# A planned attention schedule: the third branch's first pair goes by halves of the queries, and one gate projection moves to the end of the dense work

## The chip, the cores and the metric

One kernel runs on one core of a Trainium2 chip. The metric is the device time of one execution in microseconds (us); the median of three executions stands for a kernel. TensorE (PE) does the matmuls, VectorE (DVE), ScalarE (ACT) and GpSimd (POOL) the elementwise work, and SyncE's queue (SP) starts most transfers.

## The reference, cut to what matters

One decoder layer over 1024 tokens of width 1024. A projection of `x` feeds three attention branches of 8 heads of width 64, and three gates of width 1024.

```python
proj = einsum('bsd,dc->bsc', x, w_in)
o_a = dsa_attention(...)            # top 256 keys of each query by an indexer's score, then softmax
o_b = forgetting_attention(...)     # softmax with a cumulative forget bias
o_c = stick_breaking_attention(...)
up = einsum('ibsw,iwd->bsid', stack([o_a, o_b, o_c]), w_branch)
merged = sum(up * sigmoid(gates), axis=2)
y = einsum('bsd,de->bse', merged, w_out)
x = layer_norm(alpha * x + y);  x = layer_norm(alpha * x + squared_relu_mlp(x))
```

## The kernel before, in words

**Attention.** The kernel runs the branches in the order Fox (forgetting), Stick, Dsa (top-k); the third one here is Dsa. A branch has four pairs of heads, so the pairs are numbered 0 to 11 and the third branch's first pair is pair 8. The queries come in 8 row blocks of 128. A `Unit` is one head and two neighbouring row blocks: `u` from 0 to 3 has the blocks 2u and 2u+1. For each block, `qk` makes a row of scores in PSUM (tag "l", two banks; a row longer than 512 takes both), and `rows` turns it into weights `p`: a DVE operation adds the bias `bt`, reads the scores and gives the row's minimum `nm`; ACT takes the exponential with its sum `sm`; DVE inverts `sm`; POOL multiplies. Then `tr` transposes `p` (tag "t", two banks), ACT and DVE split it into `ph` and `pl`, and `pv` multiplies with `v` into tag "o".

**Selection.** `select` finds for every query its 256th largest indexer score by a bitwise search, in the background of the first two branches. At the end it handles the row blocks 2 to 7 one after the other: five DVE operations (`eq`, the scan `rk`, `eq`, `eq`, and the one that rewrites `score[i]`), and an `iota` on POOL. From `score[i]` POOL makes the bias `bt` of block i. Before a Dsa unit's scores are emitted, the loop `while selected[0] <= 2 * un.u + n` emits whatever is missing of the selection up to that block; `fill_gap` may emit more of it into a gap that the planner sees on DVE.

**Dense work.** A queue of projection tasks (`dq`) fills PE between attention steps: the q, k and v projections of the pairs (`st` is the split copy of a q or k block, which SP's queue then lays out as `qa`, `qb`, `ka`, `kb`) and the 24 gate blocks. One `gate` is a `proj_T`: 8 x 2 x 3 = 48 matmuls of 128x512 into two of the three "d" banks, then two ACT copies `g_` and two stores to `g_scratch` from ACT's queue. `GATES[4 * n + p - 1]` says how many gates follow the projections of pair 4n+p; those left over follow at the end. `dense_upto` lets the queue run ahead to the projections of the next pair. All weights of dense tasks arrive as `wraw` through SP's queue.

**Order.** `Plan` keeps an estimated clock for each engine. `drive` emits the attention step whose inputs and buffers are due, and a piece of dense work where none is due in time. The engines then run their own instructions strictly in the resulting order.

**After attention.** `load_wb` and `load_o` fetch the first branch's output (`oraw`, two halves that DVE adds, then `oh` and `ol` by ACT and DVE) into space that attention has given back. `dq.finish(len(dq.tasks))` runs what is left of the dense queue. Then the up-projections begin: for each of 8 blocks 24 matmuls with `oh`, `ol` and the weights `wbhi`, `wblo`.

In the trace almost everything has the line 138, in which the planner's helper issues an instruction; instructions are therefore told by their tiles.

Of the kernel before, what the change touches and what calls it, by code (L numbers as in the profile page):

```python
# [30 lines left out]
NPAIR = NH // 2  # L31
# [9 lines left out]

GATES = (3, 1, 3, 0, 2, 0, 2, 3, 2, 1, 2)
SLACK = 0.02
FORGET = (13, 37)
NO = 4
# [122 lines left out]
def trunk(ctx: ExitStack, tc: tile.TileContext, x, w_in, b_forget, w_branch, w_out,  # L170
# [234 lines left out]
    def swap(q):  # L405

        qs = plan.tile(ap, [P, S], F32R, tag="qs", bufs=2, name="qs")
        Q.dma_start(f32(qs[0:64]), f32(q[64:128]))
        Q.dma_start(f32(qs[64:128]), f32(q[0:64]))
        return qs  # L410
# [33 lines left out]
    def gate(br, e):  # L444
        def evac(b):
            for c, t_ in zip(HALVES, b):
                g_ = plan.tile(dp, [P, 512], F32, tag="o", bufs=NO, name="g_")
                A.activation(g_, t_, AF.Copy)
                nc.scalar.dma_start(g_dram[br, e * P:(e + 1) * P, c], g_)
        return proj_T([(0, win(OGT + br * D + e * P))], evac)  # L450
# [290 lines left out]
    for n, (oq, ok, ov) in enumerate(cols):  # L741
        for p in range(NPAIR):
# [10 lines left out]
            if (n, p) > (0, 0):  # L753
                for _ in range(GATES[4 * n + p - 1]):
                    gate(*gates.pop(0))
# [39 lines left out]
    def next_index():  # L795
        out = []
        if pend:
# [12 lines left out]
          if len(pend) > 12 else done[0])  # L810


    units = [Unit(k, 4 * n + p, pairs[4 * n + p], 2 * p + r, u) for n, k in enumerate(kinds)
             for p in range(NPAIR) for r in range(2) for u in range(4)]
    qks = [(m, n) for m in range(len(units)) for n in range(2)]
    trs = [(m, jp) for m, un in enumerate(units) for jp in range(un.u + 1)]
    st = {"qk": 0, "tr": 0, "pv": 0, "swap": 0}
    bg = select()

    def next_attention():  # L820
        out = []
        if st["pv"] < st["tr"]:
            m, jp = trs[st["pv"]]

            def pv():
                units[m].pv(jp)
                st["pv"] += 1
            out.append(Op(pv, lambda: units[m].pv_ready(jp)))
        t_m = trs[st["tr"]][0] if st["tr"] < len(trs) else len(units)
        if st["tr"] < len(trs) and st["tr"] < st["pv"] + 2 and len(units[t_m].p) == 2:  # L830
            def tr():
                units[t_m].tr()
                st["tr"] += 1
            out.append(Op(tr, units[t_m].tr_ready))
        if st["qk"] < len(qks):
            q_m, n = qks[st["qk"]]
            un = units[q_m]
            if un.kind is kinds[2]:
                hold, plan.background = plan.background, None
                while selected[0] <= 2 * un.u + n and next(bg, None) is not None:  # L840
                    pass
                plan.background = hold


            while st["swap"] <= min(q_m // 4 + 1, len(units) // 4 - 1):
                pr, r = units[4 * st["swap"]].pair, units[4 * st["swap"]].h % 2
                if "q" not in pr:
                    break
                pr["qs", r] = swap(pr["q"][r])
                st["swap"] += 1  # L850
            if q_m < t_m + 4 and dq_at() >= done[un.block]:
                def qk_():
                    un.qk()
                    st["qk"] += 1
                out.append(Op(qk_, un.qk_ready))
        out.sort(key=lambda o: o.ready())
        return out

    def dq_at():
        dq.peek()  # L860
        return dq.at
# [8 lines left out]
    def run_attention():  # L870
        while True:
            c = next_attention()
            if c:
                yield c
            elif st["pv"] >= len(trs):
                return
            else:
                dq.step()
# [97 lines left out]
    def moments(pool, z, first=True, last=True, st=None):  # L976

        if first:
            st = pool.tile([P, 2, 6], F32, tag="st", bufs=3, name="st")
            V.bn_stats(st[:, 0, :], z[:, HALVES[0]])  # L980
        if not last:
            return st
        mv = pool.tile([P, 2], F32, tag="mv", bufs=2, name="mv")
        rs = pool.tile([P, 1], F32, tag="rs", bufs=2, name="rs")
        V.bn_stats(st[:, 1, :], z[:, HALVES[1]])
        V.bn_aggr(mv, st)
        A.activation(rs, mv[:, 1:2], AF.Sqrt, bias=eps)
        return mv, rs
# [100 lines left out]
    n = NPR - 1  # L1089
# [11 lines left out]
    for i in range(NT):  # L1101
# [18 lines left out]
        st = None  # L1120
# [8 lines left out]
        for n, c in enumerate(HALVES):  # L1129
# [8 lines left out]
            st = moments(yp, rows[i], n == 0, n == 1, st)  # L1138
# [312 lines left out]
```

## Time and profile before

| | |
|---|---|
| median of 3 executions | 2062.97 us (2062.86 to 2067.82) |
| the profiled execution | 2067.44 us, span 2065.7 us |
| PE busy | 2015.8 us, 98% of the span |
| DVE / ACT / POOL busy | 67% / 48% / 23% |
| third branch's first pair (pair 8) | from about 835 to 934 us of the span |
| last attention step on PE | 1179 us |
| first up-projection matmul | 1186.8 us |

The span is the time from the first to the last instruction; 1.7 us of the execution lie outside it. A busy PE is not PE at its peak, since matmuls overlap; how far apart they start says more.

### The profile page before, as it was taken

How to read it: one execution, taken by the hardware profiler on the slowest of the kernel's cores; microseconds unless marked ns; L12 is line 12 of the kernel's file. 1: busy time of each engine (PE TensorE's matmuls, PEld its weight loads, DVE VectorE, ACT ScalarE, POOL GpSimd, SP SyncE). 2: the span in 40 equal slices, each digit the busy share in tenths (PEclk: the TensorE clock that was granted, in tenths of full speed). 3: DMA queues.
4: the chain of work that ended last, by engine and by line, in shares of the span. 5: the costliest groups of instructions: out<-in, count | busy, mean ns of one | idle time of the engine just before them, and what ended most of it. 6: DMA issues, size and time to landing. Idle time of an engine off the chain costs nothing. (4 is left out here: it accounts for less than half of the span.)

```text
span 2065.7 us, 30008 instructions
## 1 busy us (share of the span) xinstructions
PE 2015.8 (98%) x10534; PEld 1695.7 (82%) x10534; DVE 1388.8 (67%) x2501; ACT 982.3 (48%) x1913; POOL 476.8 (23%) x460
## 2 busy tenths in 40 slices
PE   8999999999999999999999999999999999999998
PEld 7788888888888888878988878887887788888886
DVE  3776387777788788854343366768787866875557
ACT  5564454444464464345344443445444455654443
POOL 3212332323353452454344204000000000000003
PEclk9999999999999999999999999999999999999999
DMA  5334434344335334243343386721699845986653
GB/s 151 89 88 103 106 99 123 87 117 105 70 93 123 72 87 108 62 107 98 83 108 87 116 284 211 246 72 42 224 342 334 305 155 184 324 281 194 192 183 122
DMA packets 210327, 308.71 MB, mean 149 GB/s; under 512 B 22248, under 2 KB 116456, under 8 KB 208128
## 3 DMA queue, kind: packets, MB, share of 16 engines
q1 hardware_dynamic: 196032, 281.09, 46.0%
q10 hardware_dynamic: 14144, 25.70, 3.5%
q8 instruction: 83, 1.36, 0.3%
q14 instruction: 68, 0.56, 0.1%
HBM read 182.89 MB, written 79.79 MB: 127 GB/s over the span
## 5 line engine op out<-in xcount | busy, mean ns | idle before, releaser
L138 PE MATMUL d<-xh,whi 128*128 128x512 f32 (+1 forms) x912 | 311.9, 401 | 12.3 <-DVE st L138 7.1
L138 PE MATMUL d<-xh,wlo 128*128 128x512 f32 (+1 forms) x912 | 305.9, 394 | 0.0
L138 PE MATMUL d<-u 128*128 128x512 f32 x1320 | 302.7, 391 | 2.3 <-ACT u L138 1.8
L138 PE MATMUL d<-xl,whi 128*128 128x512 f32 (+1 forms) x912 | 298.9, 386 | 0.0
L138 PEld LDWEIGHTS d<-u 128*128 128x128 f32 x1320 | 248.3, 188 | 56.6 <-ACT u L138 3.0
L138 POOL TENSOR_TENSOR wlo<-wraw,whi 128x512 fp32r<-128x512 f32 x138 | 193.7, 1406 | 390.5 <-ACT whi L138 293.8
L138 DVE TENSOR_TENSOR pl<-t,ph 128x512 fp32r<-128x512 f32 (+1 forms) x240 | 146.4, 630 | 90.3 <-ACT ph L138 89.9
L138 DVE TENSOR_TENSOR u<-sr,u 128x512 fp32r<-128x512 f32 x220 | 144.8, 701 | 91.0 <-ACT u L138 90.7
L138 PEld LDWEIGHTS d<-xh,whi 128*128 128x128 f32 x912 | 167.5, 191 | 40.8 <-DVE st L138 10.0
L138 PEld LDWEIGHTS d<-xl,whi 128*128 128x128 f32 x912 | 173.0, 190 | 32.4
L138 ACT ACTIVATE u<-sr 128x512 fp32r<-128x512 f32 x220 | 130.5, 627 | 140.3 <-PE d L138 104.9
L138 POOL TENSOR_TENSOR z<-z,res 128x512 f32<-128x512 f32 x14 | 19.7, 1430 | 751.9 <-ACT z L138 737.1
L138 DVE TENSOR_SCALAR_CACHE_REDUCE jk<-sc,fb 128x384 uint8<-128x384 f32 (+2 forms) x198 | 186.1, 940 | 3.4
L138 PEld LDWEIGHTS d<-xh,wlo 128*128 128x128 f32 x912 | 163.6, 190 | 25.4
L138 ACT ACTIVATE p<-p,nm 128x128 f32<-128x128 f32 (+7 forms) x128 | 99.3, 776 | 164.3 <-DVE nm L138 148.4
L138 ACT ACTIVATE ph<-t 128x512 fp32r<-128x512 f32 (+1 forms) x240 | 127.6, 558 | 95.1 <-PE t L138 90.3
L138 ACT ACTIVATE whi<-wraw 128x512 fp32r<-128x512 f32 x136 | 86.1, 633 | 175.3 <-PE d L138 103.7
L138 POOL TENSOR_SCALAR p<-p,sm 128x128 f32<-128x128 f32 (+7 forms) x128 | 97.7, 765 | 152.9 <-DVE sm L138 145.0
L138 DVE TENSOR_TENSOR_SCAN u<-u,zero 128x128 f32<-128x128 f32 (+3 forms) x64 | 110.5, 1737 | 25.5 <-ACT u L138 24.7
L138 PE MATMUL o<-ph,v 128*128 128x256 f32 x480 | 120.7, 277 | 0.0
L138 PE MATMUL o<-pl,v 128*128 128x256 f32 x480 | 118.1, 284 | 1.9 <-DVE pl L138 1.5
L138 ACT ACTIVATE mr<-mr 128x512 f32<-128x512 f32 x110 | 69.3, 630 | 92.5 <-DVE mr L138 90.5
(274 smaller groups left out, 4398.3 us busy)
## 6 DMA issues: line engine op xcount, KB each, us to landing
wraw<-in_w_in_dram SPq DMA_DIRECT2D x136, 256.0 KB, 3.0
sr<-h_scratch SPq DMA_DIRECT2D x112, 256.0 KB, 3.3
w1raw<-in_w_ff_dram SPq DMA_DIRECT2D x16, 1024.0 KB, 5.6
h_scratch<-mr SPq DMA_DIRECT2D x64, 256.0 KB, 2.9
w2raw<-in_w_ff_dram SPq DMA_DIRECT2D x16, 1024.0 KB, 7.9
t_scratch<-w2raw SPq DMA_DIRECT2D x16, 1024.0 KB, 8.9
sr<-t_scratch SPq DMA_DIRECT2D x64, 256.0 KB, 3.8
oraw<-o_scratch SPq DMA_DIRECT2D x24, 512.0 KB, 4.7
```

The lines of the kernel that those rows point to most:

```text
L138: r = f(*args, **kw)
```

## The change

`order(True)` lists the units of pair 8 as: head 0 with u = 0 and 1, head 1 with u = 0 and 1, head 0 with u = 2 and 3, head 1 with u = 2 and 3. All other pairs keep head 0 with u = 0 to 3, then head 1. `swap`, which makes a head's `qs` from its `q`, now finds pair and head by number, since a group of four units need no longer be one head. In `GATES` the entry behind pair 8's projections goes from 3 to 2; the order of the gates is the same, so every later one moves up by a place and six instead of five are left for the end.

```diff
-GATES = (3, 1, 3, 0, 2, 0, 2, 3, 2, 1, 2)
+GATES = (3, 1, 3, 0, 2, 0, 2, 2, 2, 1, 2)
...
+    def order(first):
+        return [(r, u) for v in range(2) for r in range(2) for u in (2 * v, 2 * v + 1)] if first else \
+            [(r, u) for r in range(2) for u in range(4)]
+
     units = [Unit(k, 4 * n + p, pairs[4 * n + p], 2 * p + r, u) for n, k in enumerate(kinds)
-             for p in range(NPAIR) for r in range(2) for u in range(4)]
+             for p in range(NPAIR) for r, u in order(n == 2 and p == 0)]
...
-                pr, r = units[4 * st["swap"]].pair, units[4 * st["swap"]].h % 2
+                pr, r = units[8 * (st["swap"] // 2)].pair, st["swap"] % 2
```

The planner works out a new order from this. Three places of it, with buffer numbers:

DVE behind the selection of row block 3, before. `sc4` is block 4's score; `p_9726` and `p_9776` are head 0's blocks 2 and 3. The instruction named ISA is the one with bias and minimum.

```order
L138 SCALAR_TENSOR_TENSOR sc3_93<-eq_9733,rk_9734 128x512
L138 TENSOR_SCALAR eq_9783<-sc4_94,fb_98 128x640
L138 ISA p_9726,nm_9728<-l_9721,bt_9724 128x384
L138 ISA nm_9728 128x1
L138 RECIPROCAL sm_9727<-sm_9727 128x1
L138 SCALAR_TENSOR_TENSOR rk_9784<-eq_9783,zero_66 128x640
L138 ISA p_9776,nm_9778<-l_9771,bt_9774 128x512
L138 ISA nm_9778 128x1
L138 SCALAR_TENSOR_TENSOR eq_9783<-rk_9784,need_101,eq_9783 128x640
```

The same place on DVE, changed; `p_9801` is head 1's block 0.

```order
L138 SCALAR_TENSOR_TENSOR sc3_93<-eq_9733,rk_9734 128x512
L138 ISA p_9726,nm_9728<-l_9721,bt_9724 128x384
L138 ISA nm_9728 128x1
L138 RECIPROCAL sm_9727<-sm_9727 128x1
L138 ISA p_9776,nm_9778<-l_9771,bt_9774 128x512
L138 ISA nm_9778 128x1
L138 ISA p_9801,nm_9803<-l_9794,bt_9798 128x128
L138 ISA nm_9803 128x1
L138 RECIPROCAL sm_9777<-sm_9777 128x1
L138 TENSOR_TENSOR pl_9791<-t_9786,ph_9790 128x384
L138 RECIPROCAL sm_9802<-sm_9802 128x1
L138 TENSOR_SCALAR eq_9849<-sc4_94,fb_98 128x640
```

Block 4's selection has moved behind the first steps of head 1.

DVE where head 0's block 6 (`p_9999`) meets the selection of block 7 (`sc7`), before.

```order
L138 TENSOR_SCALAR eq_10008<-sc7_97,fb_98 128x1024
L138 SCALAR_TENSOR_TENSOR rk_10009<-eq_10008,zero_66 128x1024
L138 SCALAR_TENSOR_TENSOR eq_10008<-rk_10009,need_101,eq_10008 128x1024
L138 ISA p_9999,nm_10001<-l_9991,bt_9997 128x512
L138 ISA nm_10001 128x1
L138 SCALAR_TENSOR_TENSOR eq_10008<-sc7_97,fb_98,eq_10008 128x1024
L138 ISA p_9999,nm_10003<-l_9994,bt_9997,nm_10001 128x384
```

The same place on DVE, changed; block 6 of head 0 is `p_10139` here.

```order
L138 TENSOR_SCALAR eq_10148<-sc7_97,fb_98 128x1024
L138 ISA p_10139,nm_10141<-l_10131,bt_10137 128x512
L138 ISA nm_10141 128x1
L138 SCALAR_TENSOR_TENSOR rk_10149<-eq_10148,zero_66 128x1024
L138 ISA p_10139,nm_10143<-l_10134,bt_10137,nm_10141 128x384
L138 ISA nm_10143 128x1
L138 SCALAR_TENSOR_TENSOR eq_10148<-rk_10149,need_101,eq_10148 128x1024
```

The first half of block 6's scores is now read two selection steps earlier, the second half still behind the scan.

ACT from the end of attention on, before. `wbhi` and `oh` belong to the up-projection, `g_` is a gate's copy out of PSUM.

```order
L138 ACTIVATE wbhi_13313<-wbraw_13311 128x512
L138 ACTIVATE g__13377<-d_13222 128x512
L138 ACTIVATE g__13380<-d_13251 128x512
L449 DMA g_scratch<-g__13377 128x512
L138 ACTIVATE oh_13322<-oraw_13317 128x1024
L449 DMA g_scratch<-g__13380 128x512
L138 ACTIVATE oh_13331<-oraw_13326 128x1024
L138 ACT_TABLE_LOAD
L138 ACTIVATE sg_13396<-sg_13396 128x1024
L138 ACTIVATE oh_13340<-oraw_13335 128x1024
```

The same place on ACT, changed.

```order
L138 ACTIVATE g__13321<-d_13166 128x512
L138 ACTIVATE g__13324<-d_13195 128x512
L449 DMA g_scratch<-g__13321 128x512
L138 ACTIVATE oh_13266<-oraw_13261 128x1024
L449 DMA g_scratch<-g__13324 128x512
L138 ACTIVATE oh_13275<-oraw_13270 128x1024
L138 ACT_TABLE_LOAD
L138 ACTIVATE sg_13396<-sg_13396 128x1024
L138 ACTIVATE oh_13284<-oraw_13279 128x1024
L138 ACTIVATE g__13377<-d_13327 128x512
L138 ACTIVATE g__13380<-d_13334 128x512
L449 DMA g_scratch<-g__13377 128x512
```

A second gate's copies stand between the third and the fourth `oh`. On PE, 24 dense matmuls lie between the last attention step and the first up-projection before, and 72 after the change; from the start of pair 8 to the start of pair 9 there are 280 and 246, in pair 9 344 and 330, in pair 10 198 in both, in pair 11 up to its last attention step 259 in both. The total is the same.

## Rows read from the trace of the kernel before

**Rows 1.** The page: busy time of PE over the span, and the granted TensorE clock in 40 equal slices (tenths).

```profile
PE 2015.8 (98%) x10534; PEld 1695.7 (82%) x10534; DVE 1388.8 (67%) x2501; ACT 982.3 (48%) x1913; POOL 476.8 (23%) x460
PEclk9999999999999999999999999999999999999999
```

**Rows 2.** Busy time in stretches of the span: start and end, length, then busy time (number of instructions) of PE, PEld, DVE, ACT and POOL, the granted TensorE clock as a share of 2.4 GHz, the share of the DMA engines and GB/s.

```profile
849.00:852.60 3.60, 0.01 (x2) 0.01 (x1) 2.75 (x6) 1.76 (x5) 1.73 (x2) 1.00 0.23 64
852.60:881.50 28.90, 28.90 (x135) 23.95 (x135) 23.92 (x32) 9.39 (x19) 16.29 (x14) 0.94 0.27 76
881.50:885.30 3.80, 0.01 (x2) 0.00 (x1) 3.76 (x5) 0.00 (x0) 0.59 (x1) 0.93 0.17 51
885.30:891.47 6.17, 5.66 (x13) 3.98 (x14) 4.93 (x10) 2.11 (x5) 4.81 (x6) 0.50 0.44 130
900.00:1179.00 279.00, 279.00 (x1638) 244.85 (x1637) 112.01 (x319) 130.04 (x269) 121.59 (x153) 1.00 0.40 101
1184.68:1199.29 14.61, 10.33 (x24) 5.68 (x23) 8.54 (x8) 8.73 (x10) 0.00 (x0) 0.65 0.93 301
```

**Rows 3.** Who PE waited for between 840 and 900 us: us in total, times, longest.

```profile
PE l L138 <- DVE nm L138: 4.3, 2, 3.8
PE d L138 <- ACT g__9749 L138: 3.6, 1, 3.6
```

**Rows 4.** The timeline at the first wait (start, us, engine, operation, tiles, count, and the idle time before it with its releaser), the rows of one engine after the other: PE, ACT, DVE. The first two rows are the pace of dense matmuls.

```profile
839.50 0.62 PE L138 MATMUL d<-xh,whi 128*128 128x512 f32 x2
839.96 0.61 PE L138 MATMUL d<-xl,whi 128*128 128x512 f32 x2
...
848.51 0.49 PE L138 MATMUL t<-ident,p 128*128 128x128 f32 x3
852.60 0.50 PE L138 MATMUL d<-xh,whi 128*128 128x512 f32 x1 [3.59 <-ACT g__9749 L138]
...
850.84 0.61 ACT L138 ACTIVATE p<-p,nm 128x384 f32<-128x384 f32 x1 [5.60 <-DVE nm L138]
...
851.97 0.57 ACT L138 ACTIVATE g__9749<-d 128x512 f32<-128x512 f32 x1
...
849.77 0.55 DVE L138 TENSOR_SCALAR eq<-sc,fb 128x640 uint8<-128x640 f32 x1
850.24 0.55 DVE L138 CUSTOM_DVE_ANT_0 p<-l,bt 128x384 f32<-128x384 f32 x1
...
851.57 0.16 DVE L138 RECIPROCAL sm<-sm 128x1 f32<-128x1 f32 x1 [0.77 <-ACT p L138]
```

**Rows 5.** The timeline at the second wait: PE, then DVE.

```profile
885.30 0.80 PE L138 MATMUL l<-ka,qa 128*128 128x512 f32 x1 [3.79 <-DVE nm L138]
...
887.03 0.80 PE L138 MATMUL l<-ka,qa 128*128 128x512 f32 x1 [0.51 <-DVE nm L138]
...
878.70 1.67 DVE L138 TENSOR_SCALAR eq<-sc,fb 128x1024 uint8<-128x1024 f32 x1
880.41 2.91 DVE L138 TENSOR_TENSOR_SCAN rk<-eq,zero 128x1024 f16<-128x1024 uint8 x1
...
884.55 0.68 DVE L138 CUSTOM_DVE_ANT_0 p<-l,bt 128x512 f32<-128x512 f32 x1
```

**Rows 6.** A group of DVE's instructions from 849.75 to 891.47: the tile, its shapes and count, busy time, mean ns of one, idle time before them.

```profile
L138 DVE TENSOR_TENSOR pl<-t,ph 128x512 fp32r<-128x512 f32 x2 | 1.4, 679 | 0.0
```

**Rows 7.** DVE's busy time with the tile `eq` alone (all five selection operations of a block read or write it): row blocks 4, 5, 6 and 7 in turn. Columns: stretch, length, DVE busy (instructions), clock, DMA share, GB/s.

```profile
849.77:857.30 7.53, 5.55 (x5) 0.79 0.36 111
862.90:870.12 7.22, 6.46 (x5) 1.00 0.29 94
870.12:878.66 8.54, 6.59 (x5) 1.00 0.13 32
878.70:888.64 9.94, 8.89 (x5) 0.81 0.23 62
```

**Rows 8.** The timeline: one selection operation of block 5 on DVE and the POOL operation beside it, and the same operation of block 6.

```profile
867.11 1.93 DVE L138 SCALAR_TENSOR_TENSOR eq<-sc,fb,eq 128x768 uint8<-128x768 f32 x1
...
866.23 1.99 POOL L138 TENSOR_TENSOR wlo<-wraw,whi 128x512 fp32r<-128x512 f32 x1
...
875.81 1.14 DVE L138 SCALAR_TENSOR_TENSOR eq<-sc,fb,eq 128x896 uint8<-128x896 f32 x1
```

**Rows 9.** Who PE waited for between 1180 and 1205 us.

```profile
PE d L138 <- ACT oh L138: 3.7, 3, 2.0
PE d L138 <- DVE ol L138: 0.5, 1, 0.5
```

**Rows 10.** The timeline from the last attention step to the up-projections: PE, ACT, DVE.

```profile
1179.05 0.27 PE L138 MATMUL o<-pl,v 128*128 128x128 f32 x1
...
1184.22 0.61 PE L138 MATMUL d<-xh,wlo 128*128 128x512 f32 x2
...
1198.79 0.66 PE L138 MATMUL d<-ol,wbhi 128*128 128x512 f32 x2
...
1185.70 1.06 ACT L138 ACTIVATE oh<-oraw 128x1024 fp32r<-128x1024 f32 x1
...
1196.34 1.22 DVE L138 TENSOR_TENSOR oraw<-oraw 128x1024 f32<-128x1024 f32 x1 [0.36 <-DMA oraw<-o_scratch]
1198.70 1.23 DVE L138 TENSOR_TENSOR ol<-oraw,oh 128x1024 fp32r<-128x1024 f32 x1 [0.25 <-ACT oh L138]
```

## The prediction

> **What bounds the kernel now.** I began with the page: PE is busy for 98% of the span at a granted clock of nine tenths or more in all 40 slices [rows 1]. So the total number of matmuls sets the time, and a change that keeps that number can only gain or lose where PE stands still or runs at its lower clock. The table of busy times by stretch shows where that is [rows 2]. From 900 to 1179 us PE is busy for 279.00 of 279.00 us at clock 1.00, while DVE, ACT and POOL work for 112, 130 and 122 us of it. Nothing can be gained there. Three places are left near the edit: around 849 and around 881.5 inside pair 8, and from 1184.68 at the end of attention.
>
> The list of waits names the two in pair 8: 3.6 us behind ACT's copy `g__9749`, and 4.3 us in two pieces behind DVE's `nm` [rows 3]. The timeline tells why. At 849 PE wants a "d" bank, whose copy is queued on ACT behind the exponential of a 128x384 block. That one waits for its minimum; DVE reads the scores only at 850.24, behind its selection, lastly block 4's `eq` of 0.55 us. The copy then starts at 851.97, PE at 852.60 [rows 4]. At 881.5 PE wants to write block 7's scores, but DVE has first done block 7's `eq` (1.67) and scan (2.91) and reads the scores that hold the banks only from 884.55 [rows 5].
>
> I put a price on this against PE at full speed. A dense matmul takes 0.2275 us there: two from 839.50 to 839.96 [rows 4]. Idle time is 3.6 + 3.8 + 0.5 us. The clock adds (1 - 0.94) x 28.9 = 1.7 us behind the first wait and (1 - 0.50) x 5.66 = 2.8 us behind the second, where the row shows PE at its level of 1.2 GHz [rows 2]. **Pair 8 loses 12.4 us.**
>
> At the end, 22 up-projection matmuls start between 1184.68 and 1199.29 (24 are in the row, two of them dense). At 0.2275 us they need 5.0 of the 14.6 us, so **9.6 us are lost there**: 4.2 us of waits behind `oh` and `ol` [rows 9], the rest at clock 0.65 [rows 2].
>
> **The change, the end of attention.** Call the end of the last attention matmul T0; it is 1179.16 before [rows 10]. What the up-projection waits for hangs on T0, since its copies and loads go into space and engines that attention gives back: the first `oh` starts at 1185.70 (T0 + 6.5), the fourth `oraw` has landed at 1196.34 (T0 + 17.2), the fourth `ol` ends at 1199.93 (T0 + 20.8) [rows 10]. Before, 24 dense matmuls cover 5.5 us of this; after the change 72 cover 72 x 0.2275 = 16.4 us. The first block needs its four `oh`, `ol` pairs with six matmuls each, so at T0 + 16.4, 17.8, 19.1 and 20.5. The first three are there. The fourth is late by 0.3 us if nothing moves. Its `oh` now stands behind the two copies of the last gate on ACT; the second can start only when that gate's last matmul is done at T0 + 16.4, and a copy takes about 0.6 us (`g__9749`, 0.57 [rows 4]), so ACT is free at about T0 + 17.6, before the fourth `oraw` is added up (T0 + 18.4, 1196.34 + 1.22 [rows 10]). I take 0.3 us of waiting and no loss of clock. **Gain 9.3 us.** The bounds are 9.6 and, if `oh` and `ol` come some microseconds later, half of it, since a wait here costs clock too.
>
> That the 48 matmuls are missing ahead of T0 brings no gain by itself: T0 is then 10.9 us earlier and the gate is done after it. It does need PE to be full without them. Between the starts of the pairs, 34 fewer dense matmuls are in pair 8 and 14 fewer in pair 9; pairs 10 and 11 keep theirs. In pair 9 I expect no wait, since the other engines are below half load [rows 2].
>
> **The change, pair 8.** The first wait stays, 0.5 us shorter, because block 4's `eq` of 0.55 us is no longer ahead of that read of the scores [rows 4]. I expect about 2.9 us behind the same copy.
>
> After that DVE has more to do before block 7's scores can be written, since the selection of blocks 4, 5, 6 and the first part of 7 must be done for head 0 while head 1's blocks 0 to 3 are interleaved. In DVE's new order from 849.75 to the read that frees the last bank for block 7 stand: the selection of blocks 4 to 6, 5.55 + 6.46 + 6.59 = 18.6 us [rows 7]; block 7's `eq` and scan, 1.67 + 2.91 = 4.6 [rows 5]; 12 reads of scores, from below 0.55 for the narrow ones [rows 4] to 0.68 [rows 5], I take 0.55, 6.6; six `pl`, 0.6 each by 0.68 for the widest [rows 6], 3.6; two `st`, which I price as the widest `pl`, 1.3; eight reciprocals of 0.16, 1.3 [rows 4]. That is 36.0 us. A reciprocal that follows its exponential at once finds DVE idle for 0.77 us [rows 4]; eight times this is 6.2, nothing if all are covered. One meeting with POOL on a selection step costs 0.9 (below). With 43.1 us DVE ends at **892.9**; without the idle time at 886.7.
>
> PE has less to do than that. Before, 28.9 us at clock 0.94, 27.2 at full speed, hold 135 matmuls [rows 2], of which 96 are dense: 21.8 us, and 5.4 for the 39 small ones, 0.14 each. In the new order 118 dense and 71 small matmuls stand between the first wait and the same point: 26.8 + 9.8 = 36.6 us, from 849.0 to **885.6** if PE never waited. So DVE sets the end, the first wait is paid within it, and PE loses 892.9 - 885.6 = 7.3 us. It should show as the 2.9 us above, some small waits for a bank (the transposes of head 0's block 5 need a reciprocal that stands behind block 6's `eq` and scan) and some 3 us behind block 7's scan. Behind it I keep the 2.8 us of slow clock, because what follows on DVE is the same rest of the selection. The loss is then 10.1 us instead of 12.4. **Gain 2.3 us**; bounds: 7.8 if only the first wait and its clock (2.9 + 1.7) stay, and a loss of 1.3 if four further meetings with POOL are paid.
>
> **Sum.** 9.3 + 2.3 = 11.6 us. The profiled execution took 2067.44 us and would take 2055.8; it lies 4.5 us over the median of 2062.97, so I subtract from the median: **2051.4 us**. About 0.3%, 6.2 us here, is what a measurement of this kernel can tell from no change.
>
> **Rivals.**
> - *The second wait goes.* If DVE's idle time before the reciprocals is covered by other work, it ends at 886.7, a microsecond behind PE, and PE never falls to half clock. For it: the halves put independent work of two heads next to each other. Against it: block 7's scan still stands ahead of the second read of block 6. Gain 9.3 + 7.8: 2045.9.
> - *POOL slows the selection.* One `eq` over 128x768 took 1.93 us with a POOL operation of 1.99 beside it, the wider one of block 6 alone 1.14 [rows 8]; a meeting costs about 0.9. In the changed order 28 instead of 18 POOL operations lie in this stretch. With five meetings the loss is 3.6 us more than my sum: 2055.0; with each as long as the POOL operation beside it, 5 x 1.99 = 10.0 instead of 0.9, 2060.5. The Trainium skill ("SBUF — State Buffer", section "SBUF: two separate sides") says that DVE and GpSimd share a pair of ports under an exclusive lock, so that the one that comes second is fully blocked for the other's whole instruction. By that rule the `eq` would have waited until 868.22 and, with 0.98 of its own at the wider one's rate, ended at 869.2, and the trace has 869.04: they agree to 0.2 us, and the price of the rule is the upper one.
> - *The cover at the end works by half.* The stores and copies of the last gate and the loads of `oraw` share queues. If the fourth pair is 3 us late and PE starts slow again, 4.7 us of the 9.3 remain: 2056.0.
> - *Slower: attention can't do without the 48 matmuls.* They filled places where PE would otherwise wait for the softmax, and 34 of them stood in pair 8 itself, whose gain would be gone. If all 34 + 14 leave holes, PE stands for the 10.9 us that it no longer works there, and the lower clock behind holes costs as in pair 8, 4.5 us for 7.9 us idle. That is 1.57 x 10.9 = 17.1 us against the 9.3 at the end: 7.8 slower, 2070.8. It decides from holes of 9.3 / 1.57 = 5.9 us on. Against it stand the 279 us without a wait [rows 2], in whose last two pairs nothing changes.
>
> **How the numbers follow.** Forecast 0.50 (its own range 2047 to 2056), second wait gone 0.16, POOL 0.15, half cover 0.12, holes 0.07. The predicted time is the forecast's. The range goes from 2044, below the second case, to 2061, above POOL's upper price, and leaves out the holes and some of the edges. Faster, that is below 2056.8: 0.47 of the forecast, 0.16 of the second case, 0.07 of POOL's and 0.07 of the half cover make 0.77, of which I give 0.04 to "the same" for the terms that hang on a single row; 0.73. Slower than 2069.2: 0.06. The rest, 0.21, is the same.
>
> **What would show it.** The last attention matmul should be near 1166; behind it 72 dense ones, and the first up-projection without an idle time worth naming, at clock 1.00. In pair 8 PE should wait some 2.9 us for `g__9749` or the copy that takes its place, then for `t` or `l` in pieces of 0.5 to 1.5, then some 3 us for DVE's `nm` behind block 7's scan; pair 9 should begin near 924, where it began near 934. Waits of PE from 905 on, in pair 9, would prove the fourth rival; a PE wait for `ol` over 1 us the third; selection steps above their durations here the second. I would be most wrong where the reciprocals find DVE busy, since 6.2 us hang on one row.

## The result, and the profile after

The changed kernel takes **2050.18 us** (median), the kernel before 2062.91 us in the same comparison. The ratio is 0.9932, with a 95% interval from 0.9910 to 0.9953: 14 us faster, give or take 4.5. One execution of the changed kernel (2094.7 us at a granted clock of 0.91) and one of e10 below (2574.86 us at 0.72) ran in a slower state at a lower clock and are left out of the ratios, though not out of the medians; without its slow one the changed kernel's median is 2049.24 us. The forecast was 2051.4 us, in a range from 2044 to 2061.

What PE waited for in the changed kernel, between 840 and 940 us and then from 940 to 1200. Columns: us in total, times, longest. The first two answer to [rows 3], the last to [rows 9].

```profile
PE l L138 <- DVE nm L138: 4.4, 3, 2.5
PE d L138 <- ACT g__9749 L138: 1.2, 1, 1.2
...
PE d L138 <- DVE ol L138: 0.2, 1, 0.2
```

The waits in pair 8 went from 7.9 us to 5.6, those at the end from 4.2 to 0.2. No other wait on PE appears between pair 8 and the up-projections.

Busy times of the changed kernel by stretch; the columns are those of [rows 2].

```profile
849.00:852.11 3.11, 0.62 (x5) 0.38 (x4) 2.22 (x9) 1.76 (x5) 1.91 (x5) 1.00 0.29 79
852.11:890.47 38.36, 37.70 (x187) 31.53 (x187) 29.60 (x50) 15.25 (x34) 20.81 (x23) 0.96 0.37 93
890.47:893.65 3.18, 0.73 (x2) 0.29 (x2) 3.18 (x4) 0.02 (x1) 0.46 (x1) 0.93 0.90 199
893.65:899.50 5.85, 5.85 (x20) 4.72 (x21) 4.96 (x6) 1.12 (x2) 3.47 (x3) 0.75 0.39 98
...
905.00:1165.40 260.40, 260.31 (x1542) 228.79 (x1540) 105.01 (x296) 122.12 (x252) 115.90 (x145) 1.00 0.39 99
1165.40:1187.10 21.70, 21.52 (x96) 17.49 (x95) 10.80 (x10) 11.43 (x14) 0.00 (x0) 1.00 0.76 245
```

The last row is the end of attention: PE is busy for 21.52 of 21.70 us at clock 1.00, where it had 10.33 of 14.61 at 0.65. The row above it shows that the rest of attention stays full without the 48 matmuls.

The timeline of the changed kernel, PE's first score of pair 8, the four starts after a wait in pair 8, the last attention matmul, the first up-projection and the one that waited:

```profile
834.84 0.22 PE L138 MATMUL l<-ka,qa 128*128 128x128 f32 x1
...
850.37 0.33 PE L138 MATMUL l<-kb,qb 128*128 128x128 f32 x1 [1.26 <-DVE nm L138]
...
852.11 0.70 PE L138 MATMUL d<-xh,whi 128*128 128x512 f32 x1 [1.23 <-ACT g__9749 L138]
...
890.47 0.50 PE L138 MATMUL l<-ka,qa 128*128 128x512 f32 x1 [0.66 <-DVE nm L138]
...
893.65 0.80 PE L138 MATMUL l<-ka,qa 128*128 128x512 f32 x1 [2.45 <-DVE nm L138]
...
1165.24 0.27 PE L138 MATMUL o<-pl,v 128*128 128x128 f32 x1
...
1181.75 0.62 PE L138 MATMUL d<-oh,wbhi 128*128 128x512 f32 x2
...
1186.67 0.73 PE L138 MATMUL d<-ol,wbhi 128*128 128x512 f32 x2 [0.18 <-DVE ol L138]
```

**Two sums are used from here on.** "Pairs 8 to 11" is the time from the first to the last attention matmul of pair 8 to 11 on PE: 1165.24 - 834.84 = 330.40 us here. Before it is 1179.05 [rows 10] - 834.73 (the start of the same score matmul in that trace), 344.32 us, with 48 more dense matmuls in it. To compare, each kernel's sum is brought to the changed kernel's number of dense matmuls at 0.2275 us each [rows 4]; before so counts 333.40. "Lost at the end" is the start of the 41st up-projection matmul after the last attention matmul, less the time that the dense ones and 40 more need at that pace: 24.36 - 64 x 0.2275 = 9.8 us before, 26.12 - 112 x 0.2275 = 0.6 in the changed kernel. The change is worth 3.0 us in the one and 9.2 in the other.

The two profiled executions lie 18.7 us apart, 6.5 more than that. The forecast's base had noted 4.5 us of it: the profile of before lies that far above its median, and the new one 1.5 below its own.

### The profile page after: what moved, and what is told of

It reads as the page before. It is cut to its first block, busy times and chain, and to the rows that moved or that the text cites. A ratio compares the mean times of both kernels' runs of the same rounds, so it can differ in the third digit from the quotient of the medians.

```text
span 2047.0 us, 30007 instructions
## 1 busy us (share of the span) xinstructions
PE 2005.8 (98%) x10534; PEld 1692.3 (83%) x10534; DVE 1389.8 (68%) x2501; ACT 982.0 (48%) x1913; POOL 475.8 (23%) x460
## 5 line engine op out<-in xcount | busy, mean ns | idle before, releaser
L138 ACT ACTIVATE p<-p,nm 128x896 f32<-128x896 f32 (+7 forms) x128 | 99.3, 776 | 148.4 <-DVE nm L138 132.0
L138 POOL TENSOR_SCALAR p<-p,sm 128x896 f32<-128x896 f32 (+7 forms) x128 | 98.6, 772 | 147.5 <-DVE sm L138 140.2
L138 PE MATMUL d<-whi,xh 128*128 128x256 f32 x384 | 109.5, 285 | 0.0
```

The source lines that it names most:

```text
L138: r = f(*args, **kw)
```

## The experiments

All kernels were compared with the kernel before. The table gives the ratio with its interval, both sums, the number of dense matmuls ahead of block 7's first scores (from pair 8's first score on) and the granted clock in the 11 us that begin at the first wait, for reasons told below. e9 is the changed kernel, e10 is e3, and e11 is e8, each once more.

| kernel | ratio | pairs 8 to 11 | lost at the end | dense ahead of block 7 | clock behind the first wait |
|---|---|---|---|---|---|
| before | 1 | 333.4 | 9.8 | 150 | 0.84 |
| changed | 0.9932 (0.9910 to 0.9953) | 330.4 | 0.6 | 172 | 0.84 |
| e1 order only | 0.9969 (0.9959 to 0.9979) | 326.1 | 9.9 | 195 | 0.84 |
| e2 gate only | 0.9965 (0.9950 to 0.9979) | 335.9 | 0.3 | 150 | 0.84 |
| e3 gate of pair 9 | 0.9913 (0.9895 to 0.9932) | 325.3 | 0.3 | 195 | 1.00 |
| e4 scan behind read | 0.9924 (0.9905 to 0.9943) | 329.4 | 0.9 | 172 | 0.84 |
| e5 two gates | 0.9939 (0.9921 to 0.9957) | 333.7 | 0.1 | 172 | 0.84 |
| e6 no running count | one execution, 2043.15 us | 328.5 | 0.6 | 172 | 0.84 |
| e7 two gates of pair 9 | 0.9911 (0.9889 to 0.9933) | 326.4 | 0.1 | 195 | 1.00 |
| e8 e3, read first | 0.9893 (0.9874 to 0.9913) | 325.6 | 0.3 | 195 | no wait there |
| e9 changed again | 0.9930 (0.9912 to 0.9947) | 328.8 | 0.7 | 172 | 1.00 |
| e10 e3 again | 0.9919 (0.9901 to 0.9937) | 326.9 | 0.8 | 195 | 0.84 |
| e11 e8 again | 0.9913 (0.9899 to 0.9928) | 325.4 | 0.8 | 195 | no wait there |

**e1, the order alone, and e2, the gate alone.**

```diff
e1  -GATES = (3, 1, 3, 0, 2, 0, 2, 2, 2, 1, 2)
    +GATES = (3, 1, 3, 0, 2, 0, 2, 3, 2, 1, 2)
e2  -             for p in range(NPAIR) for r, u in order(n == 2 and p == 0)]
    +             for p in range(NPAIR) for r, u in order(False)]
    ...
    -                pr, r = units[8 * (st["swap"] // 2)].pair, st["swap"] % 2
    +                pr, r = units[4 * st["swap"]].pair, units[4 * st["swap"]].h % 2
```

> The new order of pair 8 alone; the entry of GATES is 3 again, so 24 dense matmuls cover the end. The theory (two separate places): the end loses its 9.6 us as before. In pair 8, 195 instead of 172 dense matmuls now stand ahead of block 7's first scores, 5.2 us more work for PE than in the changed kernel, so the 3.1 us of waits behind DVE's nm there and the slow clock behind them (1.5 us) should be gone: pair 8 loses about 4 instead of 12.4 us, 2055 us against 2063. If the order gives only what it gave in the changed kernel (2.8 us): 2060. If the gain of the change is all of the gate: 2063.

> The gate alone; pair 8's units go head by head again. The theory: the end gives 9.3 us and pair 8 keeps its 12.4 us of loss, since its DVE order around block 7 is that of the kernel before: 2053.7. If attention cannot do without the 48 matmuls in pairs 8 and 9 (12 and 36 fewer here), holes there eat it up: 2063 or more, with PE waits in pair 9.

PE's waits between 843 and 1200 us, e1 first, then e2:

```profile
PE d L138 <- ACT oh L138: 3.1, 2, 2.0
PE l L138 <- DVE nm L138: 1.3, 1, 1.3
PE d L138 <- ACT g__9749 L138: 1.2, 1, 1.2
PE o L138 <- DVE pl L138: 1.0, 1, 1.0
PE d L138 <- DVE ol L138: 0.5, 1, 0.5
...
```

```profile
PE l L138 <- DVE nm L138: 4.8, 2, 3.8
PE d L138 <- ACT g__9749 L138: 3.6, 1, 3.6
PE d L138 <- DVE st L138: 1.0, 1, 1.0
...
```

e1 keeps the end's waits and has lost the 3.1 us ahead of block 7's scores: it gains 7.3 us in pairs 8 to 11 (333.4 to 326.1). A new wait of 1.0 us, for `pl`, stands right behind those scores. e2 has no wait at the end, and keeps both waits of pair 8, the second longer by 0.5 and followed by a new one of 1.05 for `st`: it loses 2.5 us in pairs 8 to 11, where I had expected no change. Its end gives 9.5. Both measured ratios, 6.4 and 7.2 us of 2063, agree with these sums (7.2 and 7.0). Added up, the two halves of the change are worth 14.2 us by the traces, the change itself 12.2.

So the second wait seems to depend on how much PE has to do ahead of it. The gate of 48 matmuls is part of that work. In the changed kernel the order would give 7.3 us and gives 3.0: **4.3 us of it pay for the gate that was taken out of pair 8.**

**e3, the gate taken from behind pair 9's projections, and e7, two gates from there.** If this is so, the same gate taken from a place without a bottleneck should give both gains.

```diff
e3  -GATES = (3, 1, 3, 0, 2, 0, 2, 2, 2, 1, 2)
    +GATES = (3, 1, 3, 0, 2, 0, 2, 3, 1, 1, 2)
e7  +GATES = (3, 1, 3, 0, 2, 0, 2, 3, 0, 1, 2)
```

> The new order, and the gate for the end taken from behind pair 9's projections (GATES[8] 2 to 1) instead of pair 8's (GATES[7] is 3 again). 72 dense matmuls cover the end, and 195 stand ahead of block 7's first scores as in e1. The theory: both gains in full, 9.3 + about 8, 2045.7. If DVE's chain sets the end of pair 8 whatever PE has to do there: as the changed kernel, 2050. If the 44 matmuls that pair 9 loses leave holes: 2055 or more, with PE waits in pair 9.

> The changed kernel with both gates that follow pair 9's projections moved to the end instead of one that follows pair 8's (GATES[7] 3, GATES[8] 0): 120 dense matmuls behind attention; 248 in pair 8 (276 in e3) and 280 in pair 9 (300 in e3). The theory: pair 8 is again near the changed kernel's 246, and its waits come back in part: 2046 to 2051, worse than e3 by 0 to 5. If pair 8's dense work does not matter: as e3, 2046.

All of PE's waits between 843 and 1200 us in e3:

```profile
PE l L138 <- DVE nm L138: 1.3, 1, 1.3
PE d L138 <- ACT g__9749 L138: 1.2, 1, 1.2
PE o L138 <- DVE pl L138: 1.0, 1, 1.0
```

The wait ahead of block 7's scores is gone, and so are those at the end. The timeline of e3 shows why on DVE (first three rows) and PE; the row alone below it is the same read of DVE in e10, which is e3 once more:

```profile
885.59 2.85 DVE L138 TENSOR_TENSOR_SCAN rk<-eq,zero 128x1024 f16<-128x1024 uint8 x1
...
890.53 0.60 DVE L138 CUSTOM_DVE_ANT_0 p<-l,bt,nm 128x384 f32<-128x384 f32 x1
891.07 0.08 DVE L138 DVE_READ_ACCUMULATOR2_ANT nm<- 128x1 f32 x1
...
891.97 0.40 PE L138 MATMUL l<-ka,qa 128*128 128x512 f32 x1
```

```profile
892.90 0.60 DVE L138 CUSTOM_DVE_ANT_0 p<-l,bt,nm 128x384 f32<-128x384 f32 x1
```

A rival would be that DVE itself is done sooner, since its order differs too: two `st` have moved behind the read, and a third selection operation of block 7 (1.66 us) stands ahead of it. But DVE reads block 6's second half no sooner than in the changed kernel. At the clock of 0.84 (last column of the table) it does so at 892.90 - 833.92 (the pair's first score) = 59.0 us into the pair in e10, and at 893.00 - 834.84 = 58.2 in the changed kernel; at the clock of 1.00 at 890.53 - 833.21 = 57.3 in e3, and at 890.67 - 834.07 = 56.6 in e9. PE simply has 23 more dense matmuls, 5.2 us, to do until then, and comes 0.8 us later than DVE is done. Of the 3.1 us of waiting, 1.0 comes back behind these scores, for `pl`. By the traces e3 gains 8.1 + 9.5 = 17.6 us, and 18 (14 to 22) were measured; 1.6 of the 8.1 is the clock of this one execution, as told below, and e10 gains 6.5 + 9.0 = 15.5. e7 moves a second gate. Its pair 8 has as few dense matmuls as the changed kernel (248), but still 195 of them ahead of block 7's scores, and so the wait that I expected back in part did not come: what counts is the work ahead of the wait, not in the pair. It loses 1.1 us in pairs 8 to 11 against e3, with the same three waits and 0.3 us for POOL's `p`, and gains 0.2 at the end.

**e6, the running count of block 7 left out.** This asks whether DVE's chain of work is what PE waits for, with a known piece cut out of it.

```diff
-            V.tensor_tensor_scan(rk, eq, zeros(P, w), 0.0, ALU.add, ALU.add)
+            if i < 7:
+                V.tensor_tensor_scan(rk, eq, zeros(P, w), 0.0, ALU.add, ALU.add)
+            else:
+                V.tensor_copy(rk, eq)
```

> The changed kernel, but block 7's scan over 1024 elements is replaced by a plain copy, so the running count of equal scores of that block is left out. PE's order is the same. The theory (DVE's chain of work sets when block 7's second scores are written): the chain is shorter by 2.75 us less the copy's 0.5 to 1, and PE's 2.45 us before the second scores shrink to 0 to 0.6. If something else held these banks, the wait stays.

The same place in the changed kernel (DVE), then in e6 (DVE, and PE's second scores of block 7):

```profile
890.33 2.75 DVE L138 TENSOR_TENSOR_SCAN rk<-eq,zero 128x1024 f16<-128x1024 uint8 x1
893.00 0.59 DVE L138 CUSTOM_DVE_ANT_0 p<-l,bt,nm 128x384 f32<-128x384 f32 x1
```

```profile
887.62 1.15 DVE L138 CAST rk<-eq 128x1024 f16<-128x1024 uint8 x1
888.69 0.61 DVE L138 CUSTOM_DVE_ANT_0 p<-l,bt,nm 128x384 f32<-128x384 f32 x1
...
889.36 0.50 PE L138 MATMUL l<-ka,qa 128*128 128x512 f32 x1 [0.88 <-DVE nm L138]
```

The piece became 2.75 - 1.15 = 1.60 us shorter, and PE's wait 2.45 - 0.88 = 1.57 us. The step that named DVE as the limit of this place is shown. The copy took a little more than expected, so the wait did not quite reach the range of 0 to 0.6. Not all of it is gained: 10 us later PE has a wait that the changed kernel does not have.

```profile
899.85 0.55 PE L138 MATMUL t<-ident,p 128*128 128x128 f32 x3 [1.01 <-POOL p L138]
```

The granted clock of the 5.85 us from the second scores on is 1.00 instead of 0.75, and pairs 8 to 11 gain 1.9 us in all.

**e4, the scan behind the read.** Instead of making the chain shorter, this puts block 7's five operations behind the read that PE waits for.

```diff
-                while selected[0] <= 2 * un.u + n and next(bg, None) is not None:
-                    pass
+                while selected[0] <= 2 * un.u + n:
+                    if un.u == 3:
+                        with tc.issue_after(plan.read.ins):
+                            next(bg)
+                    else:
+                        next(bg)
...
+            plan.read = V.tensor_tensor_reduce(p[:, c], l_, bias[:, c], -SCALE, m, ALU.add, ALU.min, nm)
```

> The changed kernel with the selection of block 7 held back on DVE until block 6's second half is read; the PE order is the same. The theory (PE waits 2.45 us before block 7's second scores because that read stands behind the scan of 2.75 us): this wait goes and with it the slow clock behind it (1.5 us): 2046 to 2047. The rival: block 7's score comes later by as much, its bias and first softmax too, and the wait only moves to the next step: 2050.

The four waits of PE in e4 behind the first place:

```profile
888.60 0.50 PE L138 MATMUL l<-ka,qa 128*128 128x512 f32 x1 [0.26 <-DVE nm L138]
...
889.73 0.50 PE L138 MATMUL l<-ka,qa 128*128 128x512 f32 x1 [0.40 <-DVE nm L138]
...
899.21 0.45 PE L138 MATMUL l<-kb,qb 128*128 128x384 f32 x1 [1.55 <-DVE nm L138]
...
900.48 0.38 PE L138 MATMUL l<-kb,qb 128*128 128x256 f32 x1 [0.65 <-DVE nm L138]
```

3.11 us became 0.66, and 2.20 us appeared 10 us later: block 7's score is late now, its bias and softmax with it, and head 1's scores wait for those banks. That is the rival. Pair 8's waits add up to 5.3 us, where the changed kernel has 5.6. What is left is 1.0 us in pairs 8 to 11 (330.4 to 329.4), not the 3 to 4 expected, and it is more the clock than the wait: 1.00 in the 5.85 us from block 7's first scores on, where the changed kernel has 0.75 behind its second ones. The time (0.9924) can't be told from the changed kernel's.

**e5, a second gate moved from the same place.**

```diff
-GATES = (3, 1, 3, 0, 2, 0, 2, 2, 2, 1, 2)
+GATES = (3, 1, 3, 0, 2, 0, 2, 1, 2, 1, 2)
```

> The changed kernel with a second gate moved (GATES[7] 2 to 1): 120 instead of 72 dense matmuls behind attention, 6 fewer in pair 8 and 42 fewer in pair 9. The theory: 72 already cover the end but for 0.4 us, so nothing is left to gain there; pair 9 has no selection and its engines work below half load, so the 42 missing matmuls leave few holes: 2050, as the changed kernel. The rival of the prediction (attention cannot do without its fillers): holes of up to 10.9 us in pair 9, with the lower clock up to 17: 2055 to 2067.

PE's waits in e5 between 838 and 1205 us:

```profile
PE l L138 <- DVE nm L138: 4.9, 4, 2.7
PE d L138 <- ACT g__9749 L138: 1.2, 1, 1.2
PE d L138 <- DVE st L138: 0.9, 1, 0.9
PE t L138 <- POOL p L138: 0.2, 1, 0.2
...
```

The end gains the last 0.5 us, as expected; pairs 8 to 11 lose 3.3 us against the changed kernel, where I expected few holes. They are small (0.9 for `st`, 0.3 more for block 7, two of 0.2 to 0.3 in pair 9), 1.7 us together; the other 1.6 us have no row that I could name. This is the prediction's rival of holes at a fifth of its size. e7 has the same cover at the end and takes its gates from pair 9; at 326.4, of which 1.6 us may be the clock (last column of the table), it shows that the place they leave sets the price.

**e8, the first wait removed from e3.** It holds block 3's selection back in the way of e4 (`if un.u == 1 and n == 1`), so that DVE reads head 0's block 2 ahead of it.

> e3 with block 3's selection held back on DVE until head 0's block 2 is read. In e3, DVE reads that block at 848.13 behind block 3's five operations, while its bias was there at 843.9; PE then stands 1.26 us for nm and 1.22 us for the gate's copy, and the clock falls to half for a while. The theory: ACT's exponential and with it the gate's copy come 3 to 4 us earlier and these waits go: 2.5 us and 1 to 2 us of clock less than e3, 2042 to 2043. The rival: block 3's score comes later by the read, the wait moves to block 3's scores: as e3, 2046.

All of PE's waits between 838 and 1205 us in e8:

```profile
PE o L138 <- DVE pl L138: 1.4, 2, 1.1
PE o L138 <- ACT ph L138: 0.7, 2, 0.4
PE l L138 <- DVE nm L138: 0.5, 1, 0.5
```

The 2.5 us of the first place are gone, and others stand where `ph` and `pl` come late: 2.6 us in all, where e3 had 3.5. In pairs 8 to 11 it is level with e3 (325.6 and 325.3). The clock had not fallen at that place in e3's trace (1.00), other than I wrote ahead of the run, so these two traces had no 1 to 2 us of clock to gain. Since e8's time was the lowest, three kernels were run once more:

> The changed kernel once more, beside the two that follow, on the same chip: about 12.7 us under the kernel before, as its first runs had it.

> e3 once more. If pair 8 is indeed worth 5.1 us more with the gate left in it (325.3 against 330.4 us from pair 8's first score to the end of attention in the two traces), it is 4 to 6 us under the changed kernel; if that was the luck of one execution, within 2 us of it.

> e8 once more. By its trace it should be as e3 to 1 us (the waits at pair 8's first gate copy are gone, others of the same sum stand 10 to 40 us later); if its lower median was real, it is 2 to 4 us under e3.

The ratios are 0.9930, 0.9919 and 0.9913, with intervals that overlap. The timing alone does not separate e3 from the changed kernel, or e8 from e3. The traces do so for the first pair, once the clock is looked at. The stretch of 11 us from the first wait on, in the changed kernel, in e9, in e3 and in e10:

```profile
848.90:859.90 11.00, 8.51 (x32) 6.68 (x31) 8.00 (x17) 4.40 (x11) 7.29 (x12) 0.84 0.33 96
```

```profile
848.20:859.20 11.00, 8.50 (x41) 6.89 (x40) 8.01 (x17) 4.40 (x11) 7.34 (x12) 1.00 0.33 95
```

```profile
847.30:858.30 11.00, 8.51 (x41) 6.87 (x40) 8.01 (x17) 4.40 (x11) 7.31 (x12) 1.00 0.32 95
```

```profile
848.00:859.00 11.00, 8.51 (x32) 6.66 (x31) 8.00 (x17) 4.40 (x11) 7.30 (x12) 0.84 0.32 96
```

One and the same kernel shows both clocks, with PE busy for the same 8.5 us and 41 or 32 matmuls in it. Pairs 8 to 11 differ by 1.6 us between its two executions (330.4 and 328.8; 326.9 and 325.3). At equal clocks e3 is 3.5 us below the changed kernel, both times. Of the 5.1 us expected of e10, 1.6 was the clock of one execution, and 3.5 is the gate's place. e8 and e11 have no wait there and 325.6 and 325.4, 0.6 us below the mean of e3 and e10 (326.1): no measurement here can show a gain so small.

## Why the prediction was right, point by point

**The end: right in size and in mechanism.** 9.3 us forecast, 9.2 found. The three points of time that the sum used came out: the first up-projection at 1181.75, 16.5 us after the last attention matmul started (forecast 16.4), one wait of 0.18 for `ol` (0.3), clock 1.00. e1 has its 24 matmuls of cover back and loses 9.9 again. The half cover (rival 3) is excluded: ACT's copies of the last gate did not stand in the way.

**Pair 8: right in sign, near in size (2.3 forecast, 3.0 found), the size in part by luck.** DVE's chain was to end at 892.9; its read of block 6's second half ended at 893.6. The idle time ahead of reciprocals, the term that hung on one row, was six waits of 0.73 to 1.68, 6.2 us in all; I had eight of 0.77, also 6.2. So the right sum came from a wrong count: two found DVE busy, and one took twice as long. The same holds for the whole chain. DVE's busy time in it, in the changed kernel (stretch, length, DVE busy, clock, DMA share, GB/s):

```profile
849.75:893.60 43.85, 34.31 (x59) 0.96 0.40 97
```

I had 36.9 us of work (36.0 and 0.9 for a meeting with POOL) and 6.2 of idle time. The work was 2.6 us less, and the idle time 9.5, 3.3 more: 2.0 us behind ACT's `ph` and 0.5 behind a score of PE had no term in my sum, and short pauses of DVE behind its own operations make up the rest. The two errors nearly cancel; that the end of the chain came out within 0.7 us is luck. That DVE sets it is shown by e6. The second wait was 3.11 us (forecast "some 3"). The first was 2.49, in two pieces and in part for a score bank, where I expected 2.9 in one. The small wait for the transposes did not come. The slow clock behind the second wait cost 0.25 x 5.85 = 1.5 us instead of 2.8.

**The price of the gate in pair 8 was in the sum without being seen.** I counted 118 dense matmuls ahead of the wait and found PE to be done 7.3 us before DVE. That the 48 matmuls moved away are the very work that would have filled part of this gap was not said, and the gate was costed as neutral ahead of T0 ("brings no gain by itself"). e1, which keeps the gate in pair 8, shows that taking it out costs 4.3 us there. Taken from behind pair 9's projections it costs 0.8 us at the same clock of 0.84 (326.1 in e1, 326.9 in e10), which leaves 3.5 between the two places.

**The rivals.** *The second wait goes* did not happen in the changed kernel, but does in e1, e3, e7 and e10; not because reciprocals are covered, as I had it, but because PE has more to do. *POOL*: DVE's busy time with `eq` in the changed kernel, for row blocks 4 to 7 (columns of [rows 7]):

```profile
854.72:860.75 6.03, 5.78 (x5) 0.92 0.15 44
860.75:875.25 14.50, 6.25 (x5) 1.00 0.36 90
875.25:888.25 13.00, 7.30 (x5) 1.00 0.43 95
888.25:898.70 10.45, 7.79 (x5) 0.84 0.57 135
```

That is 27.1 us, and 27.5 before [rows 7]. Block 6's selection became 0.7 us longer, block 7's 1.1 shorter: meetings with POOL changed places and did not add up. Block 6's `eq<-sc,fb,eq` took 2.06 us with a `wlo` of POOL beside it, where it had taken 1.14 [rows 8]; block 5's, which had met one and taken 1.93, took 1.02. No run took POOL's operations away, so their price stays an estimate. *Holes* was excluded for the change by its 260.31 of 260.40 us busy; e5 shows where they begin.

## What to carry to other kernels

Filler work of the bounding engine has two prices: what it covers at the place where it goes, and what it covered at the place that it leaves. Read both before it is moved, and take it from a stretch whose other engines are half idle: here the same gate cost 4.3 us in the one place and 0.8 in the other. A wait behind a chain on another engine is shortened by making the chain shorter or by giving the waiting engine more to do until then; to reorder the chain (e4, e8) moved most of the wait by some 10 to 40 us. Even the first two gave back a part: 1.0 of 1.6 us in e6 and 1.0 of 3.1 in e1 and e3 stood as new waits behind it.

## What the runs showed of the hardware that I had not expected

The clock behind a short stall is not a fixed price. The same two waits of 1.26 and 1.23 us, a few small matmuls between them, were followed by a granted clock of 0.84 over 11 us in six of the kernels' traces with that order, and by 1.00 in e3, e7 and e9, in two cases for an identical program. It is worth 1.6 us here. What decides it no run shows. A single trace's sum can so be off by more than a small edit brings, and two traces are compared at equal clocks.
